# An encoder layer in fp32: when x is summed for the seven-product form, when the second hidden block is turned, and which pool holds the attention's output

## The chip, the cores and the metric

One core of a Trainium2 chip runs the whole layer as one program. The metric is device time in microseconds. Three runs of the kernel before gave 1756.95 us as median (1756.93 to 1759.1). A core has a matrix engine (TensorE, PE), a vector engine (VectorE, DVE), a scalar engine (ScalarE, ACT), GpSimd (POOL) and a sync engine (SP). Here SP does nothing but issue DMAs, one after another in program order.

## The reference

`x` is 256 tokens by 2048. One layer is two gated feed-forward blocks (called ffn1 and ffn2 here) around an attention part:

```
x = x + 0.5 * swiglu(rms_norm(x, ffn1_norm), ffn1_w_gu, ffn1_w_down)     # 2048 -> 2 x 5632 -> 2048
h = rms_norm(x, mix_norm);  p = h @ w_in                                  # 2048 -> 4608
x = x + concat(gqa_axial(p), diff_attention(p)) @ w_out                   # 2048 -> 2048
x = x + 0.5 * swiglu(rms_norm(x, ffn2_norm), ffn2_w_gu, ffn2_w_down)
x = rms_norm(x, out_norm)
def swiglu(h): g, u = split(h @ w_gu);  return (silu(g) * u) @ w_down
```

All inputs and outputs are fp32. `rms_norm` divides a token's row by its root mean square; the kernel calls the reciprocal `rstd`.

## The kernel before

**Products.** An fp32 number is split in two fp32r parts, hi and lo. A product takes three matmuls, hi*hi, hi*lo and lo*hi (L212 to L214, and L386 to L389 in `columns`). `split` (L138) makes the parts: a copy to fp32r on ScalarE (L139) and a subtraction on VectorE (L140). Weights arrive in `raw` (four buffers of 1 MB) by DMAs on SP, and are split into `whi` and `wlo` (four buffers each). In a matmul the activations (`hT`, `xs`, `xp`, `oT`) are the 128x128 stationary operand, and the weights are the moving one, 512 wide. Results collect in six PSUM banks (`psm`); two more (`psx`) serve transposes, attention and one of the seven products.

**A feed-forward block.** The hidden width of 5632 is cut into eleven blocks of 512. Blocks 0 and 1 are computed in the plain way: the gate part (L305 to L309), then the up part (L366), whose results leave PSUM at L313 as `h`. Blocks 2 to 10 are computed by `columns(i)`, which uses a form with seven products in place of eight. For this it needs sums and differences of the normalised x, formed once by `spread`, `single_rows` and `paired_rows` (L323 to L359) into `xs` and `xp`, and sums of the weights, formed for every second pair of rows (L443 to L446, tiles `Ta` and `Tb`, then split). At the end of `columns` the products leave PSUM one by one (`done`, L394): first `p1` is copied by ScalarE (L396) to `c1`, a half of tile `sg0`, then VectorE adds the others (L392), then come SiLU and the product of the gate and up parts (L406 to L413).

**Turning.** The down product needs `h` with the hidden index on partitions. `turn_block` (L267) makes two VectorE transposes of 32x32 squares into `near` (tile `sg0`, L276), 16 moves of 32 KB from SBUF to SBUF on SP (L282), and two splits into `hT_hi` and `hT_lo` (L293). Two blocks share one pair of `hT` tiles: a group of 1024.

**Down.** `down(j, half)` multiplies group j by half of the columns of w_down and adds to x (L249). The order is `columns(2)`, `down(0, 0)`, `columns(3)`, `down(0, 1)`, and so on.

**What sets the order.** Small steps wait in the list `pending`, and `pump` takes one out at certain matmuls; `idle` is an empty step that only takes up a turn. So a step's place in the program is set by how many steps are ahead of it. In the last pair of rows of `columns` (`c == last`) all that is left is pumped (L457 to L459). A scheduler then orders each engine's instructions by its own estimate of when they can start; DMAs on SP and the steps marked `issue_after` keep to what is said there. On an engine instructions start in order: one that waits holds up all behind it.

**Names for later.** c0 to c7 are the eight pairs of rows of `columns`. `h_496` and `h_497` are blocks 0 and 1 of ffn1 before the change, `h_538` and `h_539` after it; `hT_hi_1016` and `hT_lo_1017` are the group of these two; `sg0_1229` is the `sg0` in which `c1` lies.

Of the kernel before, what the change touches and what calls it, by code (L numbers as in the profile page):

```python
# [20 lines left out]
P = 128  # L21
# [22 lines left out]
def encoder_layer(ctx: ExitStack, tc: tile.TileContext, a: dict, out: bass.AP):  # L44
# [54 lines left out]
    def pump():  # L99
        if pending:  # L100
            pending.popleft()()
# [44 lines left out]
    def rows(sets):  # L146

        def at(k, t):
            return tuple(part[:, k % 8, t * P:(t + 1) * P] for part in sets[k // 8])
        return at  # L150
# [22 lines left out]
        with tc.issue_after(loads[40].ins):  # L173
            nc.sync.dma_start(dst, src)

    def mm_block(lhs, nk, w, row0, col0, width, evac, before=None, after=None, slots=1, t_major=None):

        nb = width // 512
        nc_ = nk // 2
# [36 lines left out]
        if t_major is not None:  # L216
            with tc.manual_schedule(engines={mybir.EngineType.PE}):
                for c in range(nc_):
                    load(c)
                    for b in range(nb):  # L220
                        mm(b, 0, [2 * c, 2 * c + 1])
                        if c == nc_ - 1:
                            evac(b, 0, ps[b, 0])
                for b in range(nb):
                    step = 256 if b == nb - 1 else 512
                    for c0 in range(0, 512, step):
                        mm(b, 1, list(range(nk)), c0, c0 + step)
                        evac(b, 1, ps[b, 1], c0, c0 + step)
            return
        for c in range(nc_):  # L230
            if before is not None:
                before(c)
            load(c)
            if after is not None:
                after(c)
            n = 0
            for b in range(nb):
                for t in range(NT):
                    mm(b, t, [2 * c, 2 * c + 1])
                    n += 1  # L240
                    if n * slots // (nb * NT) > (n - 1) * slots // (nb * NT):
                        pump()
                    if c == nc_ - 1:
                        evac(b, t, ps[b, t])
# [9 lines left out]
    def ffn(xT, norm, w_gu, w_down, half_done=None, before=None, after=None, last_evac=None, last_pools=None):  # L254
# [4 lines left out]
        with tc.tile_pool(name="ffn", bufs=1) as fp:  # L259
# [37 lines left out]
                pending.append(lambda: turned_blocks.add(i))  # L297


            sg = [fp.tile([P, WB], F32, name=f"sg{t}") for t in range(NT)]  # L300

            def evac_gate(b, t, ps):
                nc.scalar.activation(sg[t][:, b * 512:(b + 1) * 512], ps, AF.Silu, scale=norm.rstd[t][:, 0:1])

            if before is None:  # L305
                mm_block(rows(xT), NK, w_gu, 0, 0, WB, evac_gate)
            else:
                with tc.manual_schedule(engines={mybir.EngineType.SP}):
                    mm_block(rows(xT), NK, w_gu, 0, 0, WB, evac_gate, lambda c: before(c, ip), after)  # L309
            h0 = [fp.tile([P, NT, 512], F32, name="h", bufs=2) for b in range(2)]  # L310

            def evac_up(b, t, ps):
                nc.vector.scalar_tensor_tensor(h0[b][:, t, :], ps, norm.rstd[t][:, 0:1],  # L313
                                               sg[t][:, b * 512:(b + 1) * 512], op0=ALU.mult, op1=ALU.mult)


            single = [k for c, pair in enumerate(PAIRS) if not pair for k in (2 * c, 2 * c + 1)]
            paired = [c for c, pair in enumerate(PAIRS) if pair]
            xs = [ip.tile([P, len(single), 3, P], F32R, name=f"xs{i}") for i in range(2)]
# [28 lines left out]
            def paired_rows(c):  # L348
# [9 lines left out]
                split(hi, lo, n.rearrange("p k t -> p (k t)")[:, :3 * P])  # L358
                split(xp[0][:, i, 3:7, :], xp[1][:, i, 3:7, :], z)  # L359

            pending.append(spread)
            pending.extend(functools.partial(paired_rows if pair else single_rows, c)
                           for c, pair in enumerate(PAIRS))
            ready = []
            pending.append(lambda: ready.append(True))
            mm_block(rows(xT), NK, w_gu, 0, DFF, WB, evac_up, slots=2)  # L366
            while not ready:
                pump()
            for b in range(2):
                turn_block(b, h0[b])  # L370


            def columns(i):
# [99 lines left out]
            def down(j, half):  # L473
                c, width = j * WB, min(WB, DFF - j * WB)
                final = j == n_groups - 1
                while not set(range(2 * j, 2 * j + width // 512)) <= turned_blocks:
                    pump()
                t_major = None
                if final and half == 1:
                    inner.close()  # L480
                    t_major = last_pools and last_pools(inner)
                evac = last_evac(half) if final and last_evac else add_to_x(half, 0.5)
                mm_block(rows([hT[j]]), width // P, w_down, c, half * WB, WB, evac, slots=2, t_major=t_major)
                if final and half_done:
                    half_done(half)

# [12 lines left out]

    def load_xT(c, pool):  # L500

        raw = pool.tile([P, 2, 512], F32, name=("Ta", "Tb")[c % 2]).rearrange("p j f -> p (j f)")[:, :2 * T]
        raw = raw.rearrange("p (j t) -> p j t", j=2)
        (nc.scalar if c == 0 else nc.sync).dma_start(raw, a["xT"][:, 2 * c:2 * c + 2, :])
        for j in range(2):
# [26 lines left out]

    raw_pool(3)
    with ExitStack() as mixer:
        mp = mixer.enter_context(tc.tile_pool(name="mix", bufs=1))
        tables = ExitStack()
        tp = tables.enter_context(tc.tile_pool(name="tables", bufs=1))
# [244 lines left out]
            return scores, probs, values, turn  # L782

        def new_oT():
            return (mp.tile([P, WB // P, T], F32R, name="oT_hi", bufs=2),
                    mp.tile([P, WB // P, T], F32R, name="oT_lo", bufs=2))

        w_in = a["w_in"]
        mm_block(rows(xT2), NK, w_in, 0, 1024, 512, evac_kva, slots=MIX_SLOTS)
# [114 lines left out]
```

## Time and profile before

| | |
|---|---|
| median of three runs | 1756.95 us |
| the profiled execution | 1757.13 us |
| its span | 1755.4 us |
| PE busy | 1731.7 us, 99% of the span |
| DVE busy | 1400.5 us, 80% |
| ACT busy | 958.3 us, 55% |
| PE's share of the chain that ended last | 90% |
| mean granted TensorE clock | 0.996 |

The span is the time from the first to the last instruction of the profiled execution; 1.7 us of its time lie around it. A matmul's row shows about 0.39 us, but the next one starts after about 0.23 us: they overlap. So what a stretch costs is read from the starts of its matmuls, and from how many of them fall into it. Where the granted clock is halved, starts are about 0.43 us apart.

### The profile page before, as it was taken

The page shows a single profiled execution, that of the slowest core. Times are in us where ns is not written, and L with a number is a line of the kernel's source. Part 1 is how long each engine was busy: PE and PEld are TensorE (multiplying, and loading weights), DVE is VectorE, ACT ScalarE, POOL GpSimd, SP SyncE. Part 2 cuts the span into 40 slices and gives each one's busy share as a digit, 9 for nine tenths or more (in the row PEclk, how much of TensorE's full clock was granted, in tenths as well). Part 3 has the DMA queues.
Part 4 walks back from the last instruction along what each step waited for, and adds up shares of the span by engine and source line. Part 5 has one row for each costly group of instructions (what it writes and reads, how often), then busy time and mean ns, then how long its engine had stood idle before and what let it go on. Part 6 is the DMA issues. An engine that isn't in the chain of part 4 may idle for free.

```text
span 1755.4 us, 21389 instructions
## 1 busy us (share of the span) xinstructions
PE 1731.7 (99%) x7652; PEld 1423.7 (81%) x7652; DVE 1400.5 (80%) x1729; ACT 958.3 (55%) x1359; POOL 48.2 (3%) x75
## 2 busy tenths in 40 slices
PE   9998999999999999999999999999999999999998
PEld 7876888888888888888788888867888888888886
DVE  6988989889889887646566565998889888988976
ACT  6555555555455554656776455555455455555544
POOL 0000000000000000122110000000000000000000
PEclk9999999999999999999999999999999999999999
DMA  9546665576566664655445455565566557656662
GB/s 368 189 161 216 212 237 193 176 248 210 183 245 204 203 209 162 219 189 196 156 173 195 145 199 184 173 232 189 202 214 220 185 201 242 205 186 240 220 227 98
DMA packets 165259, 355.81 MB, mean 203 GB/s; under 512 B 15600, under 2 KB 42656, under 8 KB 165024
## 3 DMA queue, kind: packets, MB, share of 16 engines
q1 hardware_dynamic: 164336, 353.10, 58.4%
q8 instruction: 60, 0.98, 0.2%
q10 hardware_dynamic: 720, 1.31, 0.2%
q14 instruction: 47, 0.39, 0.1%
q0 software_dynamic: 96, 0.02, 0.0%
HBM read 337.60 MB, written 2.10 MB: 194 GB/s over the span
## 4 chain that ended last, share of the span: by engine, by line
PE 90%; DMA 3%; DVE 2%; ACT 2%; SPq 2%; issue 1%; POOL 0%; POOLq 0%; ACTq 0%; DVEq 0%
PE psm L213 16%; PE psm L214 16%; PE psm L212 16%; PE psm L386 12%; PE psm L388 12%; PE psm L389 12%; DMA raw<-in_ffn_w_gu 1%; DMA raw<-in_w_in 1%; DVE wlo L140 1%; PE psx L386 1%; SPq L632 1%; PE psx L389 1%; PE psx L388 1%; DMA raw<-in_ffn_w_down 1%; SPq L282 1%
## 5 line engine op out<-in xcount | busy, mean ns | idle before, releaser
L140 DVE TENSOR_TENSOR wlo<-raw,whi 128x1024 fp32r<-128x1024 f32 (+1 forms) x644 | 713.7, 1140 | 208.3 <-ACT whi L139 204.2
L139 ACT CAST whi<-raw 128x1024 fp32r<-128x1024 f32 (+1 forms) x644 | 611.5, 984 | 480.3 <-PE psm L389 213.9
L213 PE MATMUL psm<-wlo,hT_hi 128*128 128x512 f32 x1252 | 487.8, 391 | 1.7 <-DVE wlo L140 1.7
L214 PE MATMUL psm<-whi,hT_lo 128*128 128x512 f32 x1252 | 486.3, 390 | 0.0
L212 PE MATMUL psm<-whi,hT_hi 128*128 128x512 f32 x1252 | 428.6, 391 | 4.8 <-ACT whi L139 2.1
L212 PEld LDWEIGHTS psm<-whi,hT_hi 128*128 128x128 f32 x1252 | 235.3, 188 | 56.2 <-ACT whi L139 2.9
L213 PEld LDWEIGHTS psm<-wlo,hT_hi 128*128 128x128 f32 x1252 | 235.8, 188 | 52.2 <-DVE wlo L140 3.6
L214 PEld LDWEIGHTS psm<-whi,hT_lo 128*128 128x128 f32 x1252 | 235.5, 188 | 48.2
L388 PE MATMUL psm<-wlo,xs 128*128 128x512 f32 x576 | 221.5, 390 | 0.7 <-DVE wlo L140 0.7
L389 PE MATMUL psm<-whi,xs 128*128 128x512 f32 x576 | 221.2, 389 | 0.0
L386 PE MATMUL psm<-whi,xs 128*128 128x512 f32 x576 | 196.6, 389 | 0.7 <-ACT whi L139 0.7
L388 PEld LDWEIGHTS psm<-wlo,xs 128*128 128x128 f32 x576 | 108.1, 188 | 24.2 <-DVE wlo L140 1.9
L386 PEld LDWEIGHTS psm<-whi,xs 128*128 128x128 f32 x576 | 108.0, 188 | 23.6 <-ACT whi L139 1.1
L389 PEld LDWEIGHTS psm<-whi,xs 128*128 128x128 f32 x576 | 108.1, 188 | 22.4
L139 ACT CAST Ta_hi<-Ta 128x1024 fp32r<-128x1024 f32 x72 | 75.6, 1051 | 91.0 <-DVE Ta L443 71.3
L443 DVE TENSOR_TENSOR Ta<-raw 128x1024 f32<-128x1024 f32 x72 | 87.9, 1220 | 39.2 <-DMA raw<-in_ffn_w_gu 39.0
L140 DVE TENSOR_TENSOR Tb_lo<-Tb,Tb_hi 128x1024 fp32r<-128x1024 f32 x72 | 87.8, 1219 | 2.7 <-ACT Tb_hi L139 0.8
L249 DVE SCALAR_TENSOR_TENSOR x<-psm,x 128x512 f32<-128x512 f32 (+1 forms) x113 | 73.1, 680 | 19.6 <-PE psm L214 19.4
L140 DVE TENSOR_TENSOR Ta_lo<-Ta,Ta_hi 128x1024 fp32r<-128x1024 f32 x72 | 87.7, 1219 | 0.2 <-ACT Ta_hi L139 0.2
L388 PE MATMUL psm<-wlo,xp 128*128 128x512 f32 x216 | 84.6, 392 | 0.0
L389 PE MATMUL psm<-whi,xp 128*128 128x512 f32 x216 | 84.5, 391 | 0.0
L386 PE MATMUL psm<-whi,xp 128*128 128x512 f32 x216 | 80.5, 390 | 0.4 <-ACT whi L139 0.4
(166 smaller groups left out, 1729.6 us busy)
## 6 DMA issues: line engine op xcount, KB each, us to landing
raw<-in_ffn_w_gu SPq DMA_DIRECT2D x288, 512.0 KB, 5.6
raw<-in_ffn_w_down SPq DMA_DIRECT2D x88, 1024.0 KB, 5.6
raw<-in_w_in SPq DMA_DIRECT2D x32, 1024.0 KB, 5.1
raw<-in_ffn_w_gu SPq DMA_DIRECT2D x30, 1024.0 KB, 5.9
raw<-in_w_out SPq DMA_DIRECT2D x16, 1024.0 KB, 5.0
h<-sg SPq DMA_DIRECT2D x352, 32.0 KB, 1.9
raw<-in_w_in SPq DMA_DIRECT2D x8, 512.0 KB, 3.6
heads<-near SPq DMA_DIRECT2D x96, 32.0 KB, 1.9
```

The lines of the kernel that those rows point to most:

```text
L139: casts.append(nc.scalar.copy(hi, src))
L140: return nc.vector.tensor_tensor(lo, src, f32(hi), op=ALU.subtract)
L212: nc.tensor.matmul(o, xh, wh, start=k == 0, stop=False)
L213: nc.tensor.matmul(o, xh, wl, start=False, stop=False)
L214: nc.tensor.matmul(o, xl, wh, start=False, stop=k == nk - 1)
L249: nc.vector.scalar_tensor_tensor(x[t][:, s], ps[:, c0:c1], scale, x[t][:, s], op0=ALU.mult, op1=ALU.add)
L282: nc.sync.dma_start(turned[q * B32:(q + 1) * B32, :, i_, :], near[0][i_ * B32:(i_ + 1) * B32, :, q, :])
L386: nc.tensor.matmul(bank[name], xh, wh, start=name not in begun, stop=False)
L388: nc.tensor.matmul(bank[name], xh, wl, start=False, stop=False)
L389: nc.tensor.matmul(bank[name], xl, wh, start=False, stop=end and m == n - 1)
L443: nc.vector.tensor_tensor(ta, flat[:, 3:4, :].broadcast_to([P, 2, 512]), flat[:, 1:3, :], op=ALU.subtract)
L632: nc.sync.dma_start(far[q * B32:(q + 1) * B32, i], near[i * B32:(i + 1) * B32, q].rearrange("p h d -> p (h d)"))
```

## The change

Three edits, in both feed-forward blocks where they lie in `ffn`. First, the sums of x are put into `pending` earlier: ahead of the gate part in ffn2 (where rstd is known by then), and in ffn1 after the gate part's seventh load, when the last part of x has been read. Second, the steps that turn block 1 come after six idle steps, and a `down` no longer asks for both blocks of its group at its start, but for each as its rows of w_down come up (`need`). Third, `oT_hi` and `oT_lo`, the attention's output operands, get a pool of their own. Before, these tiles begin at 137600 bytes of a partition (a multiple of 64), while `hT` begins at 67424 (32 more than a multiple of 64); after, `oT` begins at 101216, 32 more than a multiple of 64 too. Besides, loads of x in ffn1 go through three buffers in place of two.

```diff
@@ mm_block
+                    need(c)
                     load(c)
...
+            if need is not None:
+                need(c)
             load(c)
@@ ffn, ahead of the gate part
+            def form_sums():
+                pending.append(spread)
+                pending.extend(functools.partial(paired_rows if pair else single_rows, c)
+                               for c, pair in enumerate(PAIRS))
+                pending.append(lambda: ready.append(True))
+
+            def after_load(c):
+                after(c)
+                if c == 6:
+                    form_sums()
+
+            ready = []
             if before is None:
+                form_sums()
                 mm_block(rows(xT), NK, w_gu, 0, 0, WB, evac_gate)
             else:
                 with tc.manual_schedule(engines={mybir.EngineType.SP}):
-                    mm_block(rows(xT), NK, w_gu, 0, 0, WB, evac_gate, lambda c: before(c, ip), after)
+                    mm_block(rows(xT), NK, w_gu, 0, 0, WB, evac_gate, lambda c: before(c, ip), after_load, slots=2)
...
-            pending.append(spread)
-            pending.extend(functools.partial(paired_rows if pair else single_rows, c)
-                           for c, pair in enumerate(PAIRS))
-            ready = []
-            pending.append(lambda: ready.append(True))
             mm_block(rows(xT), NK, w_gu, 0, DFF, WB, evac_up, slots=2)
             while not ready:
                 pump()
-            for b in range(2):
-                turn_block(b, h0[b])
+            turn_block(0, h0[0])
+            pending.extend([idle] * 6)
+            turn_block(1, h0[1])
@@ down
-                while not set(range(2 * j, 2 * j + width // 512)) <= turned_blocks:
-                    pump()
+                def need(c):
...
+                    while 2 * j + c // 2 not in turned_blocks:
+                        pump()
...
-                mm_block(rows([hT[j]]), width // P, w_down, c, half * WB, WB, evac, slots=2, t_major=t_major)
+                mm_block(rows([hT[j]]), width // P, w_down, c, half * WB, WB, evac, slots=2, t_major=t_major, need=need)
@@ load_xT
-        raw = pool.tile([P, 2, 512], F32, name=("Ta", "Tb")[c % 2]).rearrange("p j f -> p (j f)")[:, :2 * T]
+        raw = f32(pool.tile([P, 2, 512], F32R, name=("Ta_hi", "Tb_hi", "Ta_lo")[c % 3]).rearrange("p j f -> p (j f)")[:, :2 * T])
@@ the attention part
+        ot_p = mixer.enter_context(tc.tile_pool(name="ot", bufs=2))
...
-            return (mp.tile([P, WB // P, T], F32R, name="oT_hi", bufs=2),
-                    mp.tile([P, WB // P, T], F32R, name="oT_lo", bufs=2))
+            return (ot_p.tile([P, WB // P, T], F32R, name="oT_hi"), ot_p.tile([P, WB // P, T], F32R, name="oT_lo"))
```

The number of instructions on each engine stays the same. Only their order and some addresses change. Lines of the changed kernel are a few higher: its L279 is L276 here, L285 is L282, L408 is L396, L404 is L392, L398 to L401 are L386 to L389, L455 to L458 are L443 to L446.

ScalarE in ffn1, from the last casts ahead of c7 to the copy of `p1` (L396), before:

```order
L139 CAST whi_1206<-raw_1203 128x1024
L139 CAST whi_1210<-raw_1203 128x512
L139 CAST Tb_hi_1125<-Tb_1117 128x1024
L139 CAST hT_hi_1016<-h_497 128x8x2x32 x2
L139 CAST Ta_hi_1219<-Ta_1214 128x1024
L139 CAST whi_1266<-raw_1264 128x1024
L396 COPY sg0_1229<-psm_878 128x512
```

And after, from c7's first cast on:

```order
L139 CAST Ta_hi_1198<-Ta_1193 128x1024
L139 CAST whi_1266<-raw_1264 128x1024
L139 CAST Tb_hi_1202<-Tb_1194 128x1024
L139 CAST whi_1270<-raw_1264 128x1024
L139 CAST whi_1307<-raw_1305 128x1024
L139 CAST whi_1311<-raw_1305 128x1024
L139 CAST hT_hi_1016<-h_539 128x8x2x32 x2
L408 COPY sg0_1229<-psm_878 128x512
```

Before, `hT_hi` of block 1 stands ahead of c7's casts, and one cast of down weights lies between these and the copy of `p1`. After, it stands behind all of c7's casts and behind the four casts of the first two loads of down weights, and the copy of `p1` comes right behind it. In ffn2 the rows read alike.

SP in ffn1, from the loads of c5 to the moves of block 1, before:

```order
L420 DMA raw_1105<-in_ffn1_w_gu 128x2x512 x2
L420 DMA raw_1166<-in_ffn1_w_gu 128x2x512 x2
L420 DMA raw_1203<-in_ffn1_w_gu 128x2x512 x2
L193 DMA raw_1264<-in_ffn1_w_down 128x2x1024
L282 DMA h_497<-sg0_1090 32x2x128 x16
L193 DMA raw_1305<-in_ffn1_w_down 128x2x1024
L193 DMA raw_1355<-in_ffn1_w_down 128x2x1024
L193 DMA raw_1393<-in_ffn1_w_down 128x2x1024
```

And after:

```order
L432 DMA raw_1102<-in_ffn1_w_gu 128x2x512 x2
L432 DMA raw_1147<-in_ffn1_w_gu 128x2x512 x2
L432 DMA raw_1182<-in_ffn1_w_gu 128x2x512 x2
L193 DMA raw_1264<-in_ffn1_w_down 128x2x1024
L193 DMA raw_1305<-in_ffn1_w_down 128x2x1024
L193 DMA raw_1355<-in_ffn1_w_down 128x2x1024
L193 DMA raw_1393<-in_ffn1_w_down 128x2x1024
L285 DMA h_539<-sg0_1206 32x2x128 x16
```

The 16 moves of block 1 now stand behind all four loads of down weights of `down(0, 0)`; before they stood behind the first. (In ffn2 they stood ahead of all four before.)

VectorE in ffn1 around block 1's transposes (L276, `sg0_1090<-h_497`), before:

```order
L140 TENSOR_TENSOR wlo_1071<-raw_1067,whi_1070 128x1024
L140 TENSOR_TENSOR Tb_lo_1041<-Tb_1032,Tb_hi_1040 128x1024
L140 TENSOR_TENSOR wlo_1075<-raw_1067,whi_1074 128x1024
L276 STREAM_TRANSPOSE sg0_1090<-h_497 128x512 x2
L140 TENSOR_TENSOR hT_lo_1017<-h_496,hT_hi_1016 128x8x2x32 x2
L140 TENSOR_TENSOR wlo_1109<-raw_1105,whi_1108 128x1024
L443 TENSOR_TENSOR Ta_1116<-raw_1105 128x1024
```

And after, from c7's first split to the first addition of `done` (transposes now L279):

```order
L140 TENSOR_TENSOR Ta_lo_1199<-Ta_1193,Ta_hi_1198 128x1024
L457 TENSOR_TENSOR Tb_1194<-raw_1182,Ta_1193 128x512
L458 TENSOR_TENSOR Tb_1194<-raw_1182,Tb_1194 128x512
L140 TENSOR_TENSOR wlo_1267<-raw_1264,whi_1266 128x1024
L140 TENSOR_TENSOR Tb_lo_1203<-Tb_1194,Tb_hi_1202 128x1024
L279 STREAM_TRANSPOSE sg0_1206<-h_539 128x512 x2
L140 TENSOR_TENSOR wlo_1271<-raw_1264,whi_1270 128x1024
L140 TENSOR_TENSOR wlo_1308<-raw_1305,whi_1307 128x1024
L140 TENSOR_TENSOR wlo_1312<-raw_1305,whi_1311 128x1024
L140 TENSOR_TENSOR hT_lo_1017<-h_539,hT_hi_1016 128x8x2x32 x2
L404 TENSOR_TENSOR sg1_1230<-psm_879,sg0_1229 128x512
```

Before, block 1's transposes stood right ahead of `hT_lo` of block 0, among the splits of c4 and c5. Now they stand behind the last split of c7 (`Tb_lo_1203`), and the splits of block 1 (`hT_lo`) come right ahead of the additions of `done`.

TensorE in ffn1, the end of `columns(2)` and the start of `down(0, 0)`, before:

```order
L389 MATMUL psm_877<-whi_1173,xs1_499 128x512
L386 MATMUL psx_880<-Ta_hi_1219,xp0_500 128x512
L386 MATMUL psm_874<-Ta_hi_1219,xp0_500 128x512
L212 MATMUL psm_1274<-whi_1266,hT_hi_1016 128x512
L388 MATMUL psx_880<-Ta_lo_1220,xp0_500 128x512
L389 MATMUL psx_880<-Ta_hi_1219,xp1_501 128x512
L388 MATMUL psm_874<-Ta_lo_1220,xp0_500 128x512
L389 MATMUL psm_874<-Ta_hi_1219,xp1_501 128x512
L213 MATMUL psm_1274<-wlo_1267,hT_hi_1016 128x512
```

And after:

```order
L400 MATMUL psm_874<-Ta_lo_1199,xp0_129 128x512
L401 MATMUL psm_874<-Ta_hi_1198,xp1_130 128x512
L398 MATMUL psm_879<-Tb_hi_1202,xp0_129 128x512
L398 MATMUL psm_877<-Tb_hi_1202,xp0_129 128x512
L400 MATMUL psm_879<-Tb_lo_1203,xp0_129 128x512
L401 MATMUL psm_879<-Tb_hi_1202,xp1_130 128x512
L400 MATMUL psm_877<-Tb_lo_1203,xp0_129 128x512
L401 MATMUL psm_877<-Tb_hi_1202,xp1_130 128x512
L212 MATMUL psm_1274<-whi_1266,hT_hi_1016 128x512
L213 MATMUL psm_1274<-wlo_1267,hT_hi_1016 128x512
```

Before, matmuls of `down(0, 0)` (L212 on) are woven between the last 12 of `columns(2)`; after, all of `columns(2)` comes first. The first L212 writes into the bank that `p1` leaves, and so waits for the copy at L408 (before: L396).

## Rows read from the trace of the kernel before

**Rows 1.** The page: span, and busy time of each engine

```profile
span 1755.4 us, 21389 instructions
...
PE 1731.7 (99%) x7652; PEld 1423.7 (81%) x7652; DVE 1400.5 (80%) x1729; ACT 958.3 (55%) x1359; POOL 48.2 (3%) x75
```

**Rows 2.** The engines' waits, TensorE; total us, times, longest us

```profile
PE psx L386 <- ACT Ta_hi L139: 3.1, 1, 3.1
```

**Rows 3.** Windows, TensorE; start:end, length, busy (matmuls), clock, DMA share, GB/s

```profile
88.00:176.00 88.00, 82.59 (x349) 0.98 0.55 189
180.00:268.00 88.00, 88.00 (x390) 1.00 0.64 220
1140.00:1200.00 60.00, 54.51 (x222) 0.97 0.54 180
1200.00:1260.00 60.00, 60.00 (x266) 1.00 0.64 219
```

**Rows 4.** Timeline, TensorE, ffn1; start us, us, instruction, [idle before <-releaser]

```profile
124.15 0.39 PE L386 MATMUL psm<-Ta_hi,xp 128*128 128x512 f32 x1
124.96 0.50 PE L386 MATMUL psm<-whi,xp 128*128 128x512 f32 x1 [0.41 <-ACT whi L139]
...
132.84 0.39 PE L389 MATMUL psm<-whi,xs 128*128 128x512 f32 x1
136.33 0.50 PE L386 MATMUL psx<-Ta_hi,xp 128*128 128x512 f32 x1 [3.10 <-ACT Ta_hi L139]
...
137.76 0.79 PE L212 MATMUL psm<-whi,hT_hi 128*128 128x512 f32 x1 [0.69 <-ACT sg L396]
138.35 0.63 PE L388 MATMUL psx<-Ta_lo,xp 128*128 128x512 f32 x1
138.78 0.63 PE L389 MATMUL psx<-Ta_hi,xp 128*128 128x512 f32 x1
...
140.91 0.51 PE L212 MATMUL psm<-whi,hT_hi 128*128 128x512 f32 x1
```

**Rows 5.** Timeline, ScalarE, ffn1

```profile
125.88 1.06 ACT L139 CAST Tb_hi<-Tb 128x1024 fp32r<-128x1024 f32 x1 [0.98 <-DVE Tb L446]
134.19 1.14 ACT L139 CAST hT_hi<-h 128x512 fp32r<-128x512 f32 x2 [7.25 <-DMA h<-sg]
...
137.13 0.57 ACT L396 COPY sg<-psm 128x512 f32<-128x512 f32 x1
```

**Rows 6.** Timeline, SP's DMA issues: the moves of two blocks

```profile
117.12 15.60 SPq L282 DMA_DIRECT2D h<-sg  x16
...
653.24 10.30 SPq L282 DMA_DIRECT2D h<-sg  x16
```

**Rows 7.** Timeline, VectorE, ffn1

```profile
114.65 1.30 DVE L276 STREAM_TRANSPOSE sg<-h 128x512 f32<-128x512 f32 x2
...
128.64 1.22 DVE L140 TENSOR_TENSOR Tb_lo<-Tb,Tb_hi 128x1024 fp32r<-128x1024 f32 x1
134.84 0.69 DVE L140 TENSOR_TENSOR hT_lo<-h,hT_hi 128x512 fp32r<-128x512 f32 x1 [4.99 <-ACT hT_hi L139]
```

**Rows 8.** Timeline, TensorE, second half of w_out

```profile
1000.13 0.40 PE L212 MATMUL psm<-whi,oT_hi 128*128 128x512 f32 x1
...
1002.93 0.40 PE L212 MATMUL psm<-whi,oT_hi 128*128 128x512 f32 x1
```

**Rows 9.** Timeline, TensorE, first group of ffn2's w_down

```profile
1186.70 0.39 PE L212 MATMUL psm<-whi,hT_hi 128*128 128x512 f32 x1
...
1187.83 0.39 PE L214 MATMUL psm<-whi,hT_lo 128*128 128x512 f32 x1
```

**Rows 10.** Timeline, TensorE, the program's start

```profile
1.19 3.58 PE L90 MATMUL psx<-junk 128*128 128x512 bf16 x8 [1.19 <-DVE parts L126]
```

**Rows 11.** The line of the first sum (xT hi + lo): durations, first and last start

```profile
L335 DVE TENSOR_TENSOR Ta<-hT_hi,hT_lo x16: 680/684/694, 44.9 to 1130.0; 128x512 f32<-128x512 f32 x16
```

**Rows 12.** Windows, all engines: PE, PEld, DVE, ACT, POOL busy

```profile
1140.00:1160.00 20.00, 18.59 (x80) 14.47 (x79) 19.96 (x25) 12.39 (x14) 0.00 (x0) 1.00 0.60 188
```

More of the change, by code (lines that the diff above doesn't have):

```diff
@@ L174, in late_load, with mm_block @@
             nc.sync.dma_start(dst, src)
-    def mm_block(lhs, nk, w, row0, col0, width, evac, before=None, after=None, slots=1, t_major=None):
+    def mm_block(lhs, nk, w, row0, col0, width, evac, before=None, after=None, slots=1, t_major=None, need=None):
         nb = width // 512
@@ L297, in turn_block @@
                 pending.append(lambda: turned_blocks.add(i))
[L300 to L308, printed above, removed]
-                    mm_block(rows(xT), NK, w_gu, 0, 0, WB, evac_gate, lambda c: before(c, ip), after)
[L310 to L314, printed above, removed]
             single = [k for c, pair in enumerate(PAIRS) if not pair for k in (2 * c, 2 * c + 1)]
@@ L359, in paired_rows, with evac_gate, evac_up @@
                 split(xp[0][:, i, 3:7, :], xp[1][:, i, 3:7, :], z)
-            pending.append(spread)
-            pending.extend(functools.partial(paired_rows if pair else single_rows, c)
-                           for c, pair in enumerate(PAIRS))
-            ready = []
-            pending.append(lambda: ready.append(True))
+            sg = [fp.tile([P, WB], F32, name=f"sg{t}") for t in range(NT)]
+            def evac_gate(b, t, ps):
+                nc.scalar.activation(sg[t][:, b * 512:(b + 1) * 512], ps, AF.Silu, scale=norm.rstd[t][:, 0:1])
+            def form_sums():
[7 more added lines that the diff above has]
+                    form_sums()
+            ready = []
+            if before is None:
+                form_sums()
+                mm_block(rows(xT), NK, w_gu, 0, 0, WB, evac_gate)
+            else:
+                with tc.manual_schedule(engines={mybir.EngineType.SP}):
+                    mm_block(rows(xT), NK, w_gu, 0, 0, WB, evac_gate, lambda c: before(c, ip), after_load, slots=2)
+            h0 = [fp.tile([P, NT, 512], F32, name="h", bufs=2) for b in range(2)]
+            def evac_up(b, t, ps):
+                nc.vector.scalar_tensor_tensor(h0[b][:, t, :], ps, norm.rstd[t][:, 0:1],
+                                               sg[t][:, b * 512:(b + 1) * 512], op0=ALU.mult, op1=ALU.mult)
             mm_block(rows(xT), NK, w_gu, 0, DFF, WB, evac_up, slots=2)
```

## The prediction

> **What bounds the kernel now.** I read the page first. TensorE is busy 1731.7 us of a span of 1755.4 [rows 1], and the profiled execution took 1757.13, so about 1.7 us lie around the span. So an edit counts only where it lets TensorE start matmuls earlier or later; work of other engines beside running matmuls costs nothing. Then I read TensorE's waits. The longest of all is 3.1 us, for ScalarE's cast `Ta_hi` [rows 2]; the copy L396 costs another 0.7 [rows 4]. The windows say where such time lies. Undisturbed, 88 us hold 390 matmuls and 60 us hold 266, one per 0.226 us. The 88 us around ffn1's `columns(2)` hold 349, so 41 x 0.226 = 9.3 us are lost there; the 60 us around ffn2's hold 222, so 44 x 0.226 = 9.9 us [rows 3]. These two stretches, 19.2 us in all, are what the change can win in the feed-forward blocks.
>
> The timelines give the cause in ffn1. TensorE stands from about 133 to 136.33, and meets L396 at 137.76 [rows 4]. ScalarE stood 7.25 us before that at `hT_hi` of block 1, which waits for the moves and has c7's casts behind it in the queue [rows 5]. SP began the 16 moves at 117.12 and needed 15.60 us, while a train of 16 with nothing in its way takes 10.30 [rows 6]. Two matmuls at half clock (starts at 138.35 and 138.78, 0.43 apart, 1.2 GHz in place of 2.4) show the last part of the loss: after the stand TensorE crawls until 140.91 [rows 4].
>
> **The change, part by part.**
>
> *Sums earlier.* In ffn1 the sums stand in the same order among VectorE's and ScalarE's instructions as before; the first one already started at 44.9 us [rows 11]. Value 0. In ffn2 they move forward by some ten splits of weights. VectorE is full there, 19.96 of 20 us in 1140 to 1160 [rows 12], so this relieves the small waits ahead of ffn2's long one. Those are part of the 9.9 us, which the next part replaces as a whole. One transpose for `spread` comes earlier in TensorE's queue and may hold it for up to 0.5 us, the time of a split or two; I take 0.
>
> *Turning put off.* Removed: the wait of c7's casts behind `hT_hi`, and with it, at best, all of the 9.3 and 9.9 us. Added: the whole chain of the turn, now behind c7, with L396 at its end. TensorE's first down matmul needs the bank that L396 empties, and in its queue everything else of `columns(2)` stands ahead of it. So nothing covers this chain but what is left of c7. `need` would allow two loads' worth of matmuls on block 0's rows, but they stand behind that same bank.
>
> The chain's length, from the end X of the transposes to the first down matmul: 16 moves, 10.30 us [rows 6]. From the last issue's end (117.12 + 15.60 = 132.72) to the start of `hT_hi` at 134.19 are 1.47 us [rows 5, 6]. Then `hT_hi`, 1.14 [rows 5]. Then from the start of L396 at 137.13 to the matmul at 137.76, 0.63 [rows 4, 5]. Sum 13.5 us.
>
> X in ffn1: `Tb_lo` of c5 ended at 128.64 + 1.22 = 129.86, after which VectorE stood for 4.99 us [rows 7]. In the new order the 1.30 us of transposes and one short split of 0.69 are no longer ahead of it, so it ends near 127.9. Behind it come three splits of 1.22, a short one and two short additions of 0.69 each, and the transposes of 1.30 [rows 7], 7.0 us together: X = 134.9 if VectorE never waits. The cast `Tb_hi` has one buffer, which c5's matmuls must leave first, so I take 135.0 (134 to 137). TensorE is back at 135.0 + 13.5 = 148.5. Undisturbed it would be through with `columns(2)` at 132.84 + 0.23 + 12 x 0.226, less the 0.58 lost between 124.15 and 124.96 [rows 4], that is 135.2. It stands 13.3 us.
>
> X in ffn2 has no such row. A bound holds it: c7's `Tb_hi` waits for the last matmul on c5's, behind which 22 matmuls are left (5.0 us), while the cast (1.06 [rows 5]), `Tb_lo` (1.22) and the transposes (1.30 [rows 7]) take 3.6. So X is at most 1.4 us ahead of TensorE's end, and the stand is at least 12.1 us. Above, I allow 14. I take 12.8.
>
> After each stand the clock: after 3.5 us of standing it was half from 138.35 to 140.91, six matmuls, 6 x 0.2 = 1.2 us [rows 4]; at the program's start eight matmuls at 0.43 [rows 10] make 1.6. The stand is long, so I take 1.6, between 0 and twice that.
>
> Sum: ffn1 13.3 + 1.6 + 0.2 of small waits that stay - 9.3 = +5.8; ffn2 12.8 + 1.6 - 9.9 = +4.5.
>
> *Aligned output operands.* Matmuls on `oT` start 2.80 us / 12 = 0.233 apart [rows 8], those on `hT` 1.13 / 5 = 0.226 [rows 9], with the same line, shape and weights' buffers. There are 384 on `oT`, so 384 x 0.0065 = 2.5 us, if the tile's address is the cause. It is the one difference that I see, and I take -2.5 (0 to -4; nothing speaks for a loss, as the new address has the remainder of `hT`'s). The Trainium skill, "SBUF — State Buffer", section "Operand start alignment", says that an fp32 operand need only start at a multiple of 4 bytes, and adds that this is about legality and that its runs timed nothing. Both addresses fulfil that; by the rule alone the part is worth 0. The rows show two spacings, which the rule neither explains nor forbids.
>
> *x loads through three buffers.* These loads and their casts run beside the gate part's matmuls, which wait for x at the very start alone, so 0.
>
> Total: 5.8 + 4.5 - 2.5 = +7.8; 1757.1 + 7.8 = 1764.9 us. The median of the runs is 0.2 below the profiled execution, which I leave.
>
> **Rivals.** 0.2% of the time, 3.5 us, is about what a measurement here can tell from no change.
>
> *The turn is hidden (the not-slower side).* If L396 can run before the moves have landed, TensorE goes on with block 0's rows, 48 matmuls or 10.9 us of cover, and both stretches lose nothing: 1757.1 - 19.2 - 2.5 = 1735.4. For it: the wait of 3.1 us behind `hT_hi` [rows 2] is just what the new order takes away, and `need` is written so. Against: L396 directly behind `hT_hi` in ScalarE's queue. It decides if the moves end before `p1` does, that is if the transposes come 12 us before the end of `columns(2)`; the split they stand behind rules that out. 0.10 with all that lies between it and a small gain.
>
> *The stands only replace the old ones.* At the lower bounds (12.1 in ffn2, 12.5 in ffn1, no more than 0.8 of slow clock together) the sum is 25.4 - 19.2 - 2.5 = +3.7, and with 4 for the operands +2.2: about 1760. 0.15.
>
> *The address is not the cause.* All else as forecast, no 2.5: 1767.4. For it: attention's small steps lie among these matmuls, so other engines work beside them. By the section of the Trainium skill named above this is the time to expect, since both addresses are allowed and nothing else is said of them. Against: the even 0.233 over stretches without such steps [rows 8]. 0.20.
>
> *The moves are slow again.* They now stand behind four loads of 1 MB. If the last of these lands after SP has issued half of the moves, the train takes the 15.60 us of before in place of 10.30 [rows 6], 5.3 more in each block: 1764.9 + 10.6 = 1775.5, or 1770.2 if in one. For it: this happened before, with one such load and three of the gate and up weights ahead. Against: the four loads wait for buffers that c4 to c7 leave one by one, so they are spread out. 0.10.
>
> *The change does nothing for the sums.* So it is in ffn1 by the order; it stands in the sum as 0.
>
> **How the numbers follow.** The forecast itself 0.45 (1761 to 1768 of its own); with the address rival (0.20) and the slow moves (0.10), slower by over 0.2% gets 0.75. The rival of replaced stands is within 0.2% for most of its weight: 0.14. The hidden turn and the rest give faster 0.11. The range leaves out the hidden turn below, and above the worst of the slow moves: 1754 to 1773.
>
> **What would show it.** Right: two stands of TensorE of 12 to 14 us each, one near 135, one near 1165, each ended by the copy of `p1` on ScalarE, with `hT_hi` right ahead of it waiting for the moves; a train of 16 moves of about 10.3 us inside each; half clock after both; no waits any more for `Ta_hi` and `Tb_hi`; spacing 0.226 on `oT`. Wrong: TensorE starting down matmuls while the moves still run, or a stand under 9 us, or matmuls on `oT` still 0.233 apart.

## The result, and the profile after

| | before | after |
|---|---|---|
| median of five runs | 1758.79 us (1756.93 to 1760.21) | 1775.21 us (1773.37 to 1775.83) |
| the profiled execution | 1757.13 us | 1775.83 us |
| span | 1755.4 us | 1773.9 us |
| mean granted TensorE clock | 0.996 | 0.989 |

The ratio is 1.0093, with a 95% interval of 1.0078 to 1.0108: the changed kernel is 16.4 us slower. The forecast was +7.8 us, and at most 1773 us. The direction was right, and the size was less than half of what was measured.

TensorE's waits after (total us, times, longest us), which answer to [rows 2]:

```profile
PE psm L212 <- ACT sg L408: 26.6, 2, 13.5
PE psm L213 <- DVE wlo L140: 4.5, 3, 4.0
```

The wait for `Ta_hi` is gone. In its place stand two waits for the copy of `p1`, and one that the prediction did not have, of 4.0 us for a split. TensorE's timeline after, at these three places (start us, us, instruction, idle before and its releaser):

```profile
136.73 0.40 PE L401 MATMUL psm<-Tb_hi,xp 128*128 128x512 f32 x1
150.67 0.80 PE L212 MATMUL psm<-whi,hT_hi 128*128 128x512 f32 x1 [13.54 <-ACT sg L408]
151.26 0.63 PE L213 MATMUL psm<-wlo,hT_hi 128*128 128x512 f32 x1
151.69 0.63 PE L214 MATMUL psm<-whi,hT_lo 128*128 128x512 f32 x1
...
669.50 0.79 PE L213 MATMUL psm<-wlo,hT_hi 128*128 128x512 f32 x1 [4.05 <-DVE wlo L140]
...
1182.06 0.39 PE L401 MATMUL psm<-Tb_hi,xp 128*128 128x512 f32 x1
1195.52 0.80 PE L212 MATMUL psm<-whi,hT_hi 128*128 128x512 f32 x1 [13.07 <-ACT sg L408]
...
1200.80 0.63 PE L212 MATMUL psm<-whi,hT_hi 128*128 128x512 f32 x1
1201.23 0.61 PE L213 MATMUL psm<-wlo,hT_hi 128*128 128x512 f32 x1
```

After each, matmuls start 0.43 us apart for a while, so at half clock (behind the last one until 1201.66, granted clock 0.50). The chain of the first one, on VectorE, SP and ScalarE (their timelines, in that order; they answer to [rows 5 to 7]):

```profile
135.79 1.30 DVE L279 STREAM_TRANSPOSE sg<-h 128x512 f32<-128x512 f32 x2
```

```profile
137.12 10.29 SPq L285 DMA_DIRECT2D h<-sg  x16
```

```profile
148.99 1.14 ACT L139 CAST hT_hi<-h 128x512 fp32r<-128x512 f32 x2 [11.54 <-DMA h<-sg]
150.04 0.58 ACT L408 COPY sg<-psm 128x512 f32<-128x512 f32 x1
```

From the transposes' end at 137.09 to TensorE at 150.67 are 13.6 us, and SP's issuing is 10.29 of them.

**Where the 18.5 us of the two traces lie.** Both programs have the same 7652 matmuls, so the time between matmuls of the same count can be compared, across all kernels. Worked out so from the starts in the traces, as us more than before (the runs are told below):

| kernel | start, plain blocks | `columns(2)`, ffn1 | end of ffn1 | attention part | w_out | `columns(2)`, ffn2 | all |
|---|---|---|---|---|---|---|---|
| before, us | 98.4 | 59.2 | 60.3 | 102.3 | 128.1 | 53.2 | 1745.5 |
| after | +1.9 | +6.6 | +5.8 | -1.5 | -1.8 | +6.1 | +18.5 |
| pool alone | 0 | -0.3 | +5.1 | -1.4 | -1.8 | 0 | +2.6 |
| put-off turn alone | +1.6 | +8.4 | 0 | +0.1 | 0 | +9.3 | +20.5 |
| sums alone | -0.1 | 0 | 0 | -0.1 | 0 | -4.7 | -4.2 |
| 32 bytes of pad | +0.1 | +1.6 | 0 | +0.2 | +0.1 | -1.2 | +2.6 |
| 480 bytes of pad | -0.2 | +0.1 | 0 | +0.1 | -1.7 | -0.5 | -2.0 |
| pool, tables tied | +1.3 | +1.3 | 0 | -1.4 | -1.8 | -0.6 | -1.0 |
| sums and 480 bytes | -0.2 | +0.1 | 0 | -1.4 | -1.7 | -3.6 | -5.5 |

(Stretches that differ by little stand in the last column only. The fourth is a stretch of 450 matmuls of w_in. Each row is one execution: that of the pool alone lies 2.8 us below the median of its runs, that of the put-off turn 2.2 us above.) The first column is the clock at the very start, half for eight more matmuls in the profile after; other kernels show it or not, whether their start is the old one or the new one (the put-off turn has the old start and shows it, the sums alone have the new one and do not). So about 1.9 of the 18.5 belong to this execution and not to the change, and the median is 16.4 above. The -1.4 or -1.5 in the attention part can't be put down to the pool either: the sums with 480 bytes have it too, without the new pool.

### The profile page after: what moved, and what is told of

Same layout as the page of the kernel before. It is cut to its first block, busy times and chain, and to the rows that moved or that the text cites. A ratio compares the mean times of both kernels' runs of the same rounds, so it can differ in the third digit from the quotient of the medians.

```text
span 1773.9 us, 21382 instructions
## 1 busy us (share of the span) xinstructions
PE 1729.9 (98%) x7652; PEld 1427.1 (80%) x7652; DVE 1404.0 (79%) x1729; ACT 959.5 (54%) x1359; POOL 48.1 (3%) x75
## 4 chain that ended last, share of the span: by engine, by line
PE 89%; DMA 3%; SPq 2%; DVE 2%; ACT 2%; issue 1%; POOL 0%; POOLq 0%; ACTq 0%; DVEq 0%
PE psm L213 16%; PE psm L214 16%; PE psm L212 16%; PE psm L398 12%; PE psm L400 12%; PE psm L401 12%; SPq L285 2%; DMA raw<-in_ffn_w_gu 1%; DVE wlo L140 1%; PE psx L400 1%; PE psx L401 1%; PE psx L398 1%; SPq L649 1%; DMA raw<-in_w_in 1%; ACT heads L618 0%
## 5 line engine op out<-in xcount | busy, mean ns | idle before, releaser
L212 PE MATMUL psm<-whi,hT_hi 128*128 128x512 f32 x1252 | 430.1, 393 | 29.7 <-ACT sg L408 26.6
L212 PEld LDWEIGHTS psm<-whi,hT_hi 128*128 128x128 f32 x1252 | 236.9, 190 | 80.9 <-ACT sg L408 27.5
L400 PE MATMUL psm<-wlo,xs 128*128 128x512 f32 x576 | 221.6, 390 | 0.0
L401 PE MATMUL psm<-whi,xs 128*128 128x512 f32 x576 | 221.4, 389 | 0.0
L398 PE MATMUL psm<-whi,xs 128*128 128x512 f32 x576 | 196.0, 389 | 0.0
L400 PEld LDWEIGHTS psm<-wlo,xs 128*128 128x128 f32 x576 | 108.2, 188 | 23.2 <-DVE wlo L140 0.8
L398 PEld LDWEIGHTS psm<-whi,xs 128*128 128x128 f32 x576 | 108.1, 188 | 22.5
L401 PEld LDWEIGHTS psm<-whi,xs 128*128 128x128 f32 x576 | 108.2, 188 | 22.4
L455 DVE TENSOR_TENSOR Ta<-raw 128x1024 f32<-128x1024 f32 x72 | 87.9, 1221 | 37.3 <-DMA raw<-in_ffn_w_gu 37.2
L401 PE MATMUL psm<-whi,xp 128*128 128x512 f32 x216 | 83.9, 389 | 0.0
L400 PE MATMUL psm<-wlo,xp 128*128 128x512 f32 x216 | 83.9, 389 | 0.0
L139 ACT CAST Tb_hi<-Tb 128x1024 fp32r<-128x1024 f32 x72 | 75.8, 1052 | 12.3 <-PE psm L401 6.5
```

What stands on the lines that cost most here:

```text
L139: casts.append(nc.scalar.copy(hi, src))
L212: nc.tensor.matmul(o, xh, wh, start=k == 0, stop=False)
L398: nc.tensor.matmul(bank[name], xh, wh, start=name not in begun, stop=False)
L400: nc.tensor.matmul(bank[name], xh, wl, start=False, stop=False)
L401: nc.tensor.matmul(bank[name], xl, wh, start=False, stop=end and m == n - 1)
L455: nc.vector.tensor_tensor(ta, flat[:, 3:4, :].broadcast_to([P, 2, 512]), flat[:, 1:3, :], op=ALU.subtract)
```

## The experiments

**The pool alone**

```diff
+        ot_p = mixer.enter_context(tc.tile_pool(name="ot", bufs=2))
         mp = mixer.enter_context(tc.tile_pool(name="mix", bufs=1))
...
-            return (mp.tile([P, WB // P, T], F32R, name="oT_hi", bufs=2),
-                    mp.tile([P, WB // P, T], F32R, name="oT_lo", bufs=2))
+            return (ot_p.tile([P, WB // P, T], F32R, name="oT_hi"), ot_p.tile([P, WB // P, T], F32R, name="oT_lo"))
```

> The kernel before with one edit: the attention's output operands get a pool of their own, which lies first in memory. The theory after the result: this edit moves the small operations on the rope tables (gc, gs, gsw) from the memory of sg and h to that of xs1, which comes free earlier, so they stand on VectorE ahead of block 10's additions, transposes and splits and wait there for late loads. It expects a stand of TensorE of 4 to 4.5 us near 650 at the end of ffn1, with half clock behind it, 5 to 6 us in all, spacing 0.227 on oT in place of 0.233 (-2), and +3 to +4 us over the kernel before. The rival, that the pool only changes the spacing and the stand at the end of ffn1 comes from the turn or the sums, expects -2 us and no such stand.

Measured: ratio 1.0027 (1.0013 to 1.0040), 1762.55 us beside 1757.41, so +4.7 us (2.3 to 7.0) by the ratio. The stand is there, if a little shorter than the 4 to 4.5 us expected:

```profile
660.26 0.79 PE L213 MATMUL psm<-wlo,hT_hi 128*128 128x512 f32 x1 [3.28 <-DVE wlo L140]
```

The theory holds, the rival falls: the edit that was to speed up 384 matmuls costs more than it gives. VectorE's timeline in the changed kernel shows how:

```profile
655.68 1.88 DVE L404 TENSOR_TENSOR sg<-psm,sg 128x512 f32<-128x512 f32 x3
658.52 0.30 DVE L575 COPY gsw<-bcast 128x64 f32<-128x64 f32 x2 [0.96 <-DMA bcast<-in_a_q_norm]
...
660.72 0.29 DVE L579 TENSOR_TENSOR gc_ak<-bcast,cs 128x128 f32<-128x128 f32 x1 [1.49 <-DMA bcast<-in_a_k_norm]
...
664.99 1.30 DVE L279 STREAM_TRANSPOSE sg<-h 128x512 f32<-128x512 f32 x2
...
667.98 0.33 DVE L581 COPY gc_bk<-bcast 128x96 f32<-128x96 f32 x2 [1.32 <-DMA bcast<-in_b_k_norm]
668.22 1.22 DVE L140 TENSOR_TENSOR wlo<-raw,whi 128x1024 fp32r<-128x1024 f32 x1
```

Between the additions of block 10 (L404) and the split that TensorE wants (668.22) stand 17 small operations, all but one on the rope tables, among the last steps of block 10. Each takes 0.1 to 0.3 us, but four times VectorE waits for a gain that was loaded late, and all behind it waits too. In the kernel before, the split came next after the transposes, and most of the table operations came after it:

```profile
651.90 1.30 DVE L276 STREAM_TRANSPOSE sg<-h 128x512 f32<-128x512 f32 x2
654.70 4.63 DVE L140 TENSOR_TENSOR wlo<-raw,whi 128x1024 fp32r<-128x1024 f32 x4 [1.49 <-ACT whi L139]
...
669.19 0.28 DVE L562 TENSOR_TENSOR gc_aq<-bcast,cs 128x128 f32<-128x128 f32 x1
```

By the tiles' addresses, their tables lay where `sg` lies, and could not be written before block 10 was through. The new pool takes that place, and the tables go to that of `xs1`, which is free as soon as the last products are done.

**The put-off turn alone**

```diff
-            for b in range(2):
-                turn_block(b, h0[b])
+            turn_block(0, h0[0])
+            pending.extend([idle] * 6)
+            turn_block(1, h0[1])
```

(with `need`, as in the change)

> The kernel before with one edit: block 1's turn put off by six idle steps, and need in down. The theory: two stands of TensorE of 13 to 14 us, each ended by the copy of p1, half clock behind them, +6 to +7 us in each feed-forward block, +12 to +14 us in all; nothing new at the end of ffn1; spacing on oT 0.233. The rival, that the stand at the end of ffn1 belongs to this edit (its steps shift the tables), expects +18 us and that stand here.

Measured: ratio 1.0110 (1.0096 to 1.0124), 1775.64 us. No stand at the end of ffn1, so the rival falls. Two stands as the theory has them, ScalarE's copy being at L400 here:

```profile
1155.48 0.50 PE L392 MATMUL psm<-wlo,xs 128*128 128x512 f32 x1 [0.67 <-DVE wlo L140]
...
1198.27 0.79 PE L212 MATMUL psm<-whi,hT_hi 128*128 128x512 f32 x1 [13.51 <-ACT sg L400]
```

But the price is +8.4 and +9.3 us in the two blocks in place of 6 to 7. In ffn2 the smaller waits ahead of the long one stay without the earlier sums, as the first line shows. In ffn1 ten matmuls start 0.43 us apart behind the stand, in place of six, and a wait of 0.6 us (at 123.59) stands ahead of it. So this edit by itself costs about as much as the whole change: the intervals of 1.0110 and 1.0093 overlap.

**The sums alone**

```diff
-            turn_block(0, h0[0])
-            pending.extend([idle] * 6)
-            turn_block(1, h0[1])
+            for b in range(2):
+                turn_block(b, h0[b])
```

(from the changed kernel, and its pool undone; `need` stays, and so does the `slots=2` of ffn1's gate part)

> The changed kernel with the put-off turn and the new pool undone: the sums of x earlier and three buffers for the loads of x are all that is left. The theory: nothing in ffn1; in ffn2 the waits of TensorE near 1142 and 1152 (2 us together) go, and the long one near 1166 stays; 0 to -2.5 us. The rival, that the earlier sums cost time elsewhere (the transposes of spread hold TensorE's queue at the start of ffn2, or the tables at the end of ffn1 move), expects +1 to +6 us.

Measured: ratio 0.9986 (0.9977 to 0.9996), 1754.03 us, so -2.5 us (-4.0 to -0.7); by the trace -4.2, of which -4.7 in ffn2. These are the waits of the kernel before there:

```profile
1143.07 0.73 PE L386 MATMUL psm<-whi,xs 128*128 128x512 f32 x2 [0.73 <-ACT whi L139]
1144.48 0.50 PE L388 MATMUL psm<-wlo,xs 128*128 128x512 f32 x1 [0.67 <-DVE wlo L140]
...
1168.18 0.91 PE L386 MATMUL psm<-Tb_hi,xp 128*128 128x512 f32 x2 [1.81 <-ACT Tb_hi L139]
```

The two small ones are gone, as expected (they stand at 1143 and 1144, none at 1152), and the long one too, which was not expected. The longest there is now

```profile
1168.86 0.51 PE L397 MATMUL psm<-whi,xp 128*128 128x512 f32 x1 [0.81 <-ACT whi L139]
```

and no matmul near it starts at half clock. The rival falls. That the long wait goes does not hold in every kernel with the earlier sums: with 480 bytes of pad besides (below) TensorE waits 1.93 us at 1167.24, and ffn2 gains 3.6 us.

**32 bytes of pad, and 480**

```diff
+        mp.tile([P, 8], F32, name="pad")
+
         def new_oT():
```

> The kernel before with a pad of 32 bytes ahead of the attention's output operands, in their old pool, so that they begin 32 bytes past a multiple of 64, like hT. Nothing else moves. The theory that the address sets the spacing expects 0.227 in place of 0.233 on oT, and -2 us (up to -3). The rival, that the spacing comes from attention's steps beside it and the new pool changed it in another way, expects 0.233 and no change.

> The kernel before with a pad of 480 bytes ahead of the attention's output operands in their old pool: they begin 352 past a multiple of 512, as hT, the weights' parts and the operands in the new pool do; the pad of 32 bytes left the spacing at 0.233. The theory that the remainder by 512 sets the spacing expects 0.227 and -2 us. The rival that it is not the start address within 512 bytes but the region, or what is beside, expects 0.233 and no change.

(The second has 120 in place of 8.) Measured: 32 bytes, ratio 1.0007 (0.9998 to 1.0016); 480 bytes, 0.9979 (0.9970 to 0.9988). Two stretches of the timelines, first with 32 bytes, then with 480:

```profile
1004.71 0.40 PE L212 MATMUL psm<-whi,oT_hi 128*128 128x512 f32 x1
...
1007.51 0.40 PE L212 MATMUL psm<-whi,oT_hi 128*128 128x512 f32 x1
```

```profile
989.56 0.39 PE L212 MATMUL psm<-whi,oT_hi 128*128 128x512 f32 x1
...
992.31 0.39 PE L212 MATMUL psm<-whi,oT_hi 128*128 128x512 f32 x1
```

Twelve starts take 2.80 us with 32 bytes, as before [rows 8], and 2.75 with 480; over the 366 or 367 spacings of each trace that nothing interrupts the means are 0.2333 and 0.2279. A pad of 96 bytes (the run of late splits, below) gave 0.2327. So the start address does set the spacing, and not by its remainder by 64 or 128: of the starts tried, those 352 past a multiple of 512 are fast (the new pool, and 480 bytes), and those 384, 416 and 480 past it are not. `hT` and the weights' parts all start at 352. Whether it counts that the two operands agree, or what each is, was not tried.

**Half of the moves in a second queue**

```diff
-                        nc.sync.dma_start(turned[q * B32:(q + 1) * B32, :, i_, :],
+                        (nc.scalar if i == 1 and q % 2 else nc.sync).dma_start(turned[q * B32:(q + 1) * B32, :, i_, :],
```

(in the changed kernel)

> The changed kernel with one edit: of the 16 moves of block 1 (that block alone), 8 are issued by ScalarE's queue in place of SP's, beside the other 8. The theory that the stand is the length of the chain from the transposes to the copy of p1, of which SP's issuing is 10.3 us: the trains take some 5 us in place of 10.3, both stands of 13.5 us shrink to about 8.5, and the time falls by 9 to 11 us. The rival that the moves are bound by what carries them (the DMA engines, beside loads of 1 MB) and not by the issuing: the stands keep 12 to 13.5 us and the time falls by less than 3 us.

Measured: 1764.81 us, ratio to before 1.0036 (1.0024 to 1.0049), so 10.4 us less than the changed kernel by the medians, and 10.0 by the two ratios. SP's and ScalarE's queues, and TensorE behind them:

```profile
135.37 5.46 SPq L285 DMA_DIRECT2D h<-sg  x8
```

```profile
135.38 5.81 ACTq L285 DMA_DIRECT2D h<-sg  x8
```

```profile
144.19 0.80 PE L212 MATMUL psm<-whi,hT_hi 128*128 128x512 f32 x1 [8.80 <-ACT sg L408]
```

The stand in ffn2 fell to 8.97 us. The stand is the chain, and the chain is mostly SP's issuing: halving it took 4.7 us from the stand of 13.54. The Trainium skill, "DMA: Bandwidth & Descriptors", section "Issuing engines are not separate DMA queues", says that issuing on several engines saves only the time of issuing, which is usually small beside the DMA. The trace agrees with the first half: the time of issuing is what was saved. One issue of 0.6 us is small here too, beside a landing of 1.9 us; but 16 of them stand one behind the other, and their 10.3 us are not.

**More buffers for the gains, and the tables tied**

```diff
-            t_ = tp.tile([P, n], F32, name=f"bcast{n}", bufs=1 if n > HD else 2)
+            t_ = tp.tile([P, n], F32, name=f"bcast{n}", bufs=1 if n > HD else 4)
```

> The kernel before with the attention's new pool, as in the run of the pool alone, and four buffers in place of two for the rows of q and k gains that the table operations read (bcast128). The theory that the stand of 3.7 us at the end of ffn1 is VectorE waiting in order for late loads, which themselves wait for a buffer that an earlier table operation reads: these loads are issued early here, the stand falls under 1.5 us, and the time is 3 to 4 us under that of the pool alone. The rival that the table operations' own number and time ahead of the transposes and splits makes the stand: it keeps 3 us or more, no gain.

Measured: ratio 1.0015 (1.0006 to 1.0024), 1762.00 us, against 1.0027 for the pool alone; the intervals overlap. The stand fell only from 3.28 to 2.85:

```profile
659.01 0.50 PE L213 MATMUL psm<-wlo,hT_hi 128*128 128x512 f32 x1 [2.85 <-DVE wlo L140]
```

But the edit did not take the waits for loads away. They add up to 3.5 us on VectorE here, in place of 3.9 with the pool alone; the longest of the four is

```profile
651.02 0.29 DVE L563 TENSOR_TENSOR gc_ak<-bcast,cs 128x128 f32<-128x128 f32 x1 [1.47 <-DMA bcast<-in_a_k_norm]
```

So the two buffers are not the main reason of these waits, and that part of my theory falls. How much of the stand is waiting for loads, and how much the operations' own time, this run does not decide. The place of the operations is then tested by itself:

```diff
         rope = {}
-        for grp, nrot, hs in (("a", HD, 32), ("b", B_ROT, 16)):
+        with tc.issue_after(splits[-1].ins):
+            for grp, nrot, hs in (("a", HD, 32), ("b", B_ROT, 16)):
...
```

(around all of the table operations, in the kernel with the pool alone)

> The kernel before with the attention's new pool, and the table operations tied behind the last split of ffn1, so that on VectorE they stand behind block 10's transposes and splits again. The theory that the pool's cost is the place of these operations ahead of the splits expects no stand at the end of ffn1, 0.228 on oT, and -2 to -4 us against the kernel before. The rival that the work and the late loads only move their wait (to the start of the attention part, where the tables are read) expects a new stand of 2 us or more near 710 and no gain.

Measured: ratio 0.9989 (0.9981 to 0.9998), 1756.20 us. No stand at the end of ffn1, none near 710 either. VectorE there:

```profile
653.41 1.30 DVE L276 STREAM_TRANSPOSE sg<-h 128x512 f32<-128x512 f32 x2
657.49 4.63 DVE L140 TENSOR_TENSOR wlo<-raw,whi 128x1024 fp32r<-128x1024 f32 x4 [2.77 <-ACT whi L139]
```

So the 5 us come from the place of these operations ahead of the splits, and the pool by itself put them there. That it did so through the memory that comes free earlier is read from the addresses and not tested apart.

**Late splits**

```diff
-                pending.extend([turn, idle] + [functools.partial(move, i0) for i0 in (0, 2)] + [idle])
+                pending.extend([turn, idle] + [functools.partial(move, i0) for i0 in (0, 2)] + [idle] * (1 + late))
...
+                    with tc.issue_after(casts[-1].ins):
+                        casts.append(nc.scalar.copy(hi, src))
```

(the sums alone, the turn at its old place; `late` is 6 for block 1; with 96 bytes of pad)

> The kernel with the sums alone, and: the turn at its old place, but block 1's splits (hT_hi, hT_lo) held back by six idle steps and tied behind the casts made so far, and the attention's operands pushed by 96 bytes in their old pool (96 past a multiple of 128, as hT). The theory that the wait of before is the place of hT_hi on ScalarE, ahead of c7's casts, and not the turn: -3 to -5 us in ffn1 and -2 to -3 in ffn2 against the sums alone, no stand over 3 us, about 1746 to 1750. The rival that the copy of p1 keeps it, since c1 lies in the tile that the moves read and so waits for them wherever hT_hi stands: TensorE resumes as late as before, within 2 us of the sums alone (1752 to 1755). For the operands: 0.227 if the remainder by 128 sets the spacing, else 0.233.

Measured: ratio 0.9982 (0.9973 to 0.9990), 1755.14 us, not clearly different from the sums alone. The rival holds. ScalarE in ffn1:

```profile
135.89 0.59 ACT L409 COPY sg<-psm 128x512 f32<-128x512 f32 x1 [2.81 <-DMA h<-sg]
...
141.86 1.04 ACT L139 CAST Tb_hi<-Tb 128x1024 fp32r<-128x1024 f32 x1
142.81 1.13 ACT L296 CAST hT_hi<-h 128x512 fp32r<-128x512 f32 x2
```

With `hT_hi` behind it, the copy still waits for the moves, since it writes the tile they read, and c7's `Tb_hi` stands behind the copy.

**What paid, together**

> The two parts that paid by themselves, together: the sums earlier (with three buffers for the loads of x), and 480 bytes of pad in place of the new pool. No put-off turn. If the parts add up: -4 for the sums by the trace and -2 for the spacing, 1750 to 1753, faster than both kernels. The rival that they share their gain (the clock after the stands decides): no better than the sums alone.

Measured: ratio 0.9966 (0.9954 to 0.9978), 1751.99 us: faster than both kernels, and about the sum of the two parts.

> As the run of the sums and the pad, and of block 1's 16 moves 8 on ScalarE's queue, at the old place of the turn. The theory that the 15.6 us of moves in one queue made the old waits too: the moves are done some 5 us earlier, hT_hi stands behind c7's casts, the long wait near 133 and that near 1168 fall under 1.5 us each, and the time is 5 to 10 us under the run of the sums and the pad (1741 to 1747). The rival: the moves on ScalarE wait in order behind each other for landed loads and hold its casts up, as long or longer than before: no gain, or slower.

> As the last, with GpSimd's queue for the 8 moves in place of ScalarE's. The theory that it is the issuing in one queue: as good as with ScalarE's queue or better, since GpSimd has nothing else to do there. The rival that its DMAs take longer from issue to landing: hT_hi starts no earlier than before and the time stays that of the sums and the pad.

Measured: with ScalarE's queue 0.9978 (0.9969 to 0.9987), 1754.63 us; with GpSimd's 0.9956 (0.9944 to 0.9969), 1751.43 us. ScalarE's queue, then SP's and GpSimd's of the other kernel:

```profile
119.65 5.20 ACTq L285 DMA_DIRECT2D h<-sg  x3
124.98 1.04 ACT L139 CAST Ta_hi<-Ta 128x1024 fp32r<-128x1024 f32 x1 [4.73 <-DMA raw<-in_ffn_w_gu]
```

```profile
116.35 12.84 SPq L285 DMA_DIRECT2D h<-sg  x8
```

```profile
116.21 4.29 POOL L285 DMA_DIRECT2D h<-sg  x8 [78.53 <-DVE sg L279]
```

On ScalarE the moves hold its casts up, as the rival had it: three take 5.20 us. On GpSimd eight are issued in 4.29 us, but SP's own eight still take 12.84, so here it is not the number of issues. In ffn1 the kernel with GpSimd's queue gained 2.1 us and lost as much later by the trace; against the sums and the pad its interval decides nothing. In ffn2 the kernel with ScalarE's queue gained 5.8 us by the trace, beside 3.6 for the sums and the pad, so the second queue did not only cost; by the medians it is no better, and the two intervals overlap.

## Why the prediction was wrong

*What bounds, and the chain: right.* TensorE came back 13.6 us after the transposes' end (forecast 13.5), with SP's train of 10.29 inside, `hT_hi` and the copy behind it. The waits for `Ta_hi` and `Tb_hi` went. The stands were 13.5 and 13.1 us by their waits (13.3 and 12.8 forecast). So every sign that was to show the forecast right came, but for the spacing of 0.228 in place of 0.226, and none of those against it: the signs looked only at the parts that had been thought of.

*The step that failed: "Aligned output operands".* It said "-2.5 (0 to -4; nothing speaks for a loss, as the new address has the remainder of `hT`'s)". It priced the tile's own matmuls and not what the tile pushes aside. The gain came, -1.8 us, and for the reason meant (a start address), though by another remainder. (The rows of the prediction give 0.2333 - 0.226 = 0.0073 and 2.8 us, where it wrote 0.0065 and 2.5; the new spacing was 0.228.) But the pool cost +5.1 (alone) to +5.8 us (in the change) at the end of ffn1, shown by the pool alone and by its going when the tables are tied. The rows of order under the change showed only `columns(2)`; the same comparison of VectorE's order at the end of ffn1 held the answer, since table operations stand there ahead of the transposes.

*Mis-sized: the clock behind the second stand, 1.6 us.* In ffn1 it is 0.36 + 6 x 0.2 = 1.6, as forecast; in ffn2, 13 matmuls at 0.43 make 0.36 + 13 x 0.2 = 3.0. By the starts each stand cost 0.4 us more than forecast (13.94 and 13.46 less one spacing of 0.23), and the turn cost 6.6 + 6.1 = 12.7 in place of 10.3.

*The sums: right in ffn1, where nothing moved, too small in ffn2.* I took their value as replaced by the turn; by themselves they are worth 4.7 us in ffn2 by the trace, and beside the turn the difference of +9.3 and +6.1 is 3.2.

*The sum.* Forecast +5.8 + 4.5 - 2.5 = 7.8. By the trace 6.6 + 6.1 - 1.8 + 5.8 = 16.7, then -1.5 (fewer matmuls at half clock in the attention part), +1.9 (the start) and 1.4 in small pieces: 18.5. The missing term and the clock are 7.2 of the 10.7 that the forecast lacked, and 1.9 of the rest are this execution's start.

*Rivals.* The slow moves did not come (10.29 and 10.30); their 1775.5 us lie beside the measured 1775.2 by chance. The address was the cause. The hidden turn failed where it was said to: the copy stood behind the moves. The stands did not merely replace the old waits: both were longer than the lower bounds of that rival.

## What to carry to other kernels

Before giving a buffer a new pool, ask which tiles lose their old place: memory that comes free earlier lets a scheduler pull small operations forward, into the queue of the engine that feeds the matmuls. A step that is put off to get it out of the way ends up at the head of the next wait, if the stage's end needs it (here through a shared tile); its chain is then paid in full, and so is the half clock behind it. Edits that are made together should be timed apart: of three here one paid, one took more than it gave, and one by itself cost about as much as all three.

## What the runs showed of the hardware

The start address of the stationary operand changed the spacing of fp32r matmuls by 2.4%: 0.2331 us at 384 bytes past a multiple of 512, 0.2333 at 416, 0.2327 at 480, and 0.228 at 352. The Trainium skill, "SBUF — State Buffer", section "Operand start alignment", speaks of what is legal alone; all four are.

Starts 0.43 us apart behind a stand lasted for 6 matmuls where two starts lay 13.9 us apart, and for 13 where they lay 13.5 apart. In the attention part a gap of 2.2 us between starts was followed by 8 of them in the kernel before and by 1 in the kernel after. So in these traces the length of the gap does not set their number.
